# The second layer's output projection as seven block products, its weight blocks prepared during the first FFN

## The chip, the cores and the metric

The kernel runs on one core of one Trainium2 chip. The metric is the device time of one execution in microseconds (us), the median of several runs. The engines named below are PE (TensorE, the matrix multiplier), DVE (VectorE), ACT (ScalarE), POOL (GpSimd) and SP (SyncE); SP starts transfers on hardware queues, POOL starts them on a software queue, and only the latter are used here for transfers that add into their destination.

## The reference, cut to what matters

A decoder trunk of two layers on 1024 tokens with 1024 channels, all in float32. What matters here is the output projection `merged @ w_o[l]` and its surroundings:

```
for l in range(2):
    h = rmsnorm(x, norm1[l]);  proj = h @ w_in[l]          # q, k, v of two mixers, and two gates
    o_a, o_b = two attention mixers
    merged = g_a * (o_a @ w_br[l, :OUT_A]) + g_b * (o_b @ w_br[l, OUT_A:])
    x = x + merged @ w_o[l]                                 # 1024 x 1024 by 1024 x 1024
    h2 = rmsnorm(x, norm2[l]);  up = h2 @ w_up[l]           # 1024 x 5632
    x = x + (gelu(conv(a)) * v) @ w_down[l]                 # 2816 x 1024
return rmsnorm(x, norm_f)
```

## The kernel before, in words

**Arithmetic.** A float32 matrix product is made of three matmuls in PE's faster float32 format: each operand is split into a high part (a cast on ACT, `w_hi`, `hh`, `t_hi`) and a low part, the rest (a subtraction on DVE, `w_lo`, `hl`, `t_lo`; line 152 in `split`). Then hi·hi, hi·lo and lo·hi are added in one PSUM bank. One matmul has 128 weight columns against 512 tokens.

**Block products.** Most of the large products (the input projection, FFN up, FFN down) are already made in blocks of two by two, with seven block products and sums of blocks instead of eight block products. The output projection is not: `wo_chunk` makes one of 16 chunks, token half `n` by output block `e`, from 8 plain block pairs, thus 24 matmuls a chunk and 384 a layer. For each chunk, the weights of `w_o` are loaded (`w_raw`, two transfers of 256 KB), split on ACT and DVE, multiplied, and the result in PSUM is added to the residual `x` on DVE (line 1321). Then `norm_add` squares it on ACT and adds the square to `nrm` on DVE (line 491).

**The norm behind it.** When all eight chunks of a token half are done, four matmuls with `ones` (`nrm_t`) sum `nrm` over the channels, ACT and DVE make 1/sqrt of it (`ss`), and four matmuls (`nrm_b`) spread it over the partitions. DVE then scales `x` (`b_f`, line 563), ACT casts `hh` and DVE subtracts `hl`. In the second layer, `first_half()` does this for token half 0, and the sums of blocks for the FFN behind it (`s`, `t_hi`, `t_lo`), beside the chunks of half 1: `drive` mixes the two by a ratio. The norm of half 1 is left over as `pending` and is mixed into the first units of the FFN (`u_ps`).

**The branch stage ahead of it.** The two attention outputs go through `w_br` (`br_ps`), are multiplied by the gates (`gin`), added (`mrg`) and split: `hh` on ACT, `hl` on POOL (line 1419). Gates come from DRAM (`gs` to `gin`), as does the residual `x` (`xs`, 1 MB a transfer).

**The first FFN.** Units 2 to 21 of `up` make FFN up. Each unit has 84 matmuls in 14 steps of 6. In it, raw weights come by SP (`up_a<-in_w_up_dram`), are combined by DVE and by one adding transfer of POOL (line 1651, `up_a<-up_a`), are split on ACT and DVE, and ACT carries results out of PSUM (`u<-u_a`, `u<-u_c`) so that the bank can be used again.

**What sets the order.** Within these units PE, ACT, DVE and POOL run their instructions in the order of the program text (`IN_ORDER`); elsewhere a scheduler sets the order of ACT, DVE, POOL and SP, and SP's order throughout. Each engine runs its own list in order, and waits at the head of it.

Of the kernel before, what the change touches and what calls it, by code (L numbers as in the profile page):

```python
# [7 lines left out]
F32 = mybir.dt.float32  # L8
# [22 lines left out]
EPS = 1e-6  # L31
GRP = 2
NRAW = 2
PT = 6
WARM = 3
GROUPS = (2, 2, 3, 4)
# [23 lines left out]
def f32(ap):  # L60
    return ap.bitcast(F32)
# [3 lines left out]
def trunk_kernel(ctx, tc, x, xt, head0, norm1, vecs, w_in, w_br, w_o, w_up, w_down, norm_f, out, depth=None, probe=None):  # L65
# [57 lines left out]
    sq = [dr.tile([2, 2, 64, T], F32, name=f"sq{i}") for i in range(4)]  # L123
    sv = [dr.tile([P, n, KD, P], F32, name=f"sv{n}") for n in (4, 2, 2)]
    dn = [dr.tile([4, T], F32, name=f"dn{i}") for i in range(2)]
    fd = dr.tile([4, T], F32, name="fd")
# [62 lines left out]
    def drive(side, main, ratio, lead=0):  # L189

        due = 0.0
        for _ in range(lead):
            next(main, 0)
        for _ in side:
            due += ratio
            while due >= 1.0:
                due -= 1.0
                if next(main, 0) == 0:
                    due = -1e9
        for _ in main:  # L200
            pass
# [239 lines left out]
    def h_part(n, k):  # L441
        return H[n][0][:, k, :], H[n][1][:, k, :]
# [9 lines left out]
    def xc(n, e, sub=slice(0, HF)):  # L452
        return X[n][e // 4][:, e % 4, sub]
# [12 lines left out]
    def x_in(l, n, h):  # L466

        if h == 0:
            X[n] = [None, None]
        X[n][h] = quarter(f"x{n}")  # L470
        k = slice(4 * h, 4 * h + 4)
        if l:
            nc.sync.dma_start(X[n][h], xs[n][:, k, :])
        elif n:
            nc.sync.dma_start(X[n][h], x_first(1, HF, T)[:, k, :])
        else:
            for a in range(0, HF, 2 * P):
                nc.sync.dma_start(X[n][h][:, :, a : a + 2 * P], x_first(0, a, a + 2 * P)[:, k, :])
# [1 line left out]

    ACC = [None, None]

    def norm_add(n, e, first=False):

        if first:
            ACC[n] = sb.tile([P, HF], F32, tag="ql", bufs=2, name="nrm")
        acc = ACC[n]
        sq = acc if first else small("sq")
        act.activation(sq, xc(n, e), AF.Square)
        if not first:  # L490
            dve.tensor_tensor(acc, acc, sq, ALU.add)
# [824 lines left out]
    def wo_chunk(l, n, e):  # L1316
        w = weights(w_o[l][:, e * P : (e + 1) * P], P)
        yield
        o = bank("ps", "o_ps")
        yield from product(o, [(w[k], h_part(n, k)) for k in range(KD)])  # L1320
        dve.tensor_tensor(xc(n, e), xc(n, e), o, ALU.add)
        norm_add(n, e, e == 0)
        yield

    def mixer(l, pending):
        R.clear()
        dense = Dense()
# [79 lines left out]
        def branch_in(i):  # L1407
            if i < len(todo):
# [5 lines left out]
                    split(*parts_[q], raw[:, 2 * q : 2 * q + 2, :])  # L1414
                wbs.append(parts_)

        def merged(n, e, m):
            act.copy(H[n][0][:, e, :], m)
            pool.tensor_tensor(H[n][1][:, e, :], m, f32(H[n][0][:, e, :]), ALU.subtract)

        wo = [wo_chunk(l, n, e) for n in range(2) for e in range(KD)]

        for i in range(3):
            gate_load(i)
# [11 lines left out]
        for i, ab in order:  # L1436
            n, e = todo[i]
            sl = slice(n * HF, (n + 1) * HF)
            if i not in seen:
                if e == 0:  # L1440
                    new_h(n)
                if i % 4 == 0:
                    wb = wbs.pop(0)
                if i in X_AT:
                    late_x = X_AT.index(i)
                    x_in(l, late_x // 2, late_x % 2)
            gt = gts[i]
            ec = slice((e % 2) * P, (e % 2 + 1) * P)
            o = bank("s" if ab and i < 2 else (("ps", "s"), ("t", "o"))[ab][i // 2 % 2], "br_ps")
            (wh, wl), (xh, xl) = wb[ab], oh["ab"[ab]]  # L1450
            for _ in product(o, [((wh[:, c, ec], wl[:, c, ec]), (xh[:, c, sl], xl[:, c, sl])) for c in range(2)]):
                pass
            with tc.high_priority(offset=AHEAD):
                dve.tensor_tensor(gt[:, ab, :], gt[:, ab, :], o, ALU.mult)
            seen[i] = seen.get(i, 0) + 1
            if seen[i] == 1:
                continue
            m = small("mrg")
            dve.tensor_tensor(m, gt[:, 0, :], gt[:, 1, :], ALU.add)
            late.append((n, e, m))  # L1460
# [5 lines left out]
            if i == 12:  # L1466
                next(wo[0])
        merged(*late.pop(0))
        table(AF.Sqrt, gt[:, 1, 0:1])
# [2 lines left out]
        def first_half():  # L1472
            yield from norm(0, g2[:, 0, :], "t", keep=True)
            yield from first_sum()

        drive(first_half(), relay(*wo, primed=True), 2.5, 36)
        return norm(1, g2[:, 0, :], "t", AF.Gelu, True)

    def ffn(l, pending, final):
# [106 lines left out]
        def before(steps, n):  # L1586

            while now[1] < n and next(steps, 0) != 0:
                yield
# [12 lines left out]
        def up_weights(j, vv):  # L1602
            return weights(w_up[l][:, vv * DFF + j * P : vv * DFF + (j + 1) * P], P)

        def up_plain(j, order, turns, extra):

            yield
            yield
            w = [up_weights(j, 0), up_weights(j, 1)]
# [269 lines left out]
        for _ in steps:  # L1879
            pass  # L1880
        return box[0]

    heads = {}

    def enter(l):

# [457 lines left out]
```

## Time and profile before

| | before |
|---|---|
| median of 3 runs | 2594.13 us (2591.62 to 2595.03) |
| the profiled execution's own time | 2593.59 us |
| its span, first to last instruction | 2591.8 us |
| busy PE / DVE / ACT / POOL | 2577.4 / 2061.1 / 1334.1 / 130.0 us |
| granted TensorE clock | 1.0 |
| share of the DMA engines' time, hardware / software queue | 56.0% / 2.7% |

The profiled execution lies 0.54 us under the median, and 1.8 us of it lie outside the span. An engine's busy time is counted over the span, so PE was idle for 14.4 us in all. In the tables by stretch, each engine has its busy time and, in brackets, the number of its instructions; the last columns are the granted clock, the busy share of the 16 DMA engines, and GB/s. In a timeline a row has its start, its length and, in square brackets, the engine's idle time before it and what ended that.

### The profile page before, as it was taken

The page shows a single profiled execution, that of the slowest core. Times are in us where ns is not written, and L with a number is a line of the kernel's source. Part 1 is how long each engine was busy: PE and PEld are TensorE (multiplying, and loading weights), DVE is VectorE, ACT ScalarE, POOL GpSimd, SP SyncE. Part 2 cuts the span into 40 slices and gives each one's busy share as a digit, 9 for nine tenths or more (in the row PEclk, how much of TensorE's full clock was granted, in tenths as well). Part 3 has the DMA queues.
Part 4 walks back from the last instruction along what each step waited for, and adds up shares of the span by engine and source line. Part 5 has one row for each costly group of instructions (what it writes and reads, how often), then busy time and mean ns, then how long its engine had stood idle before and what let it go on. Part 6 is the DMA issues. An engine that isn't in the chain of part 4 may idle for free.

```text
span 2591.8 us, 35872 instructions
## 1 busy us (share of the span) xinstructions
PE 2577.4 (99%) x12536; PEld 2153.4 (83%) x12536; DVE 2061.1 (80%) x3410; ACT 1334.1 (51%) x2488; POOL 130.0 (5%) x175
## 2 busy tenths in 40 slices
PE   9999999999999999999999999999999999999999
PEld 8888888888888888888888888888888888888887
DVE  8878877796878878897677788778868888879966
ACT  6555566664554545432445555666645555544223
POOL 1000000030000000000000000000300000000000
PEclk9999999999999999999999999999999999999999
DMA  7434579863355455688344436798634455457963
GB/s 261 152 114 145 158 197 233 235 224 105 103 158 166 155 186 155 246 323 312 147 149 147 127 129 188 199 242 235 198 99 129 138 174 164 157 184 251 347 241 134
DMA packets 402579, 480.02 MB, mean 185 GB/s; under 512 B 25272, under 2 KB 311392, under 8 KB 400736
## 3 DMA queue, kind: packets, MB, share of 16 engines
q1 hardware_dynamic: 395776, 464.85, 56.0%
q0 software_dynamic: 6464, 12.62, 2.7%
q8 instruction: 99, 1.62, 0.3%
q14 instruction: 80, 0.66, 0.1%
q10 hardware_dynamic: 160, 0.27, 0.0%
HBM read 308.74 MB, written 158.43 MB: 180 GB/s over the span
## 4 chain that ended last, share of the span: by engine, by line
PE 92%; DVE 4%; ACT 2%; DMA 1%; issue 1%; POOL 0%; DVEq 0%; ACTq 0%; POOLq 0%
PE u_a L1053 5%; PE u_a L1052 5%; PE u_a L1054 5%; PE d_ps L1801 5%; PE d_ps L1802 5%; PE d_ps L1803 5%; PE i_a L1052 5%; PE i_a L1053 5%; PE i_a L1054 5%; PE u_c L1052 3%; PE u_c L1053 3%; PE u_c L1054 3%; PE i_c L1052 2%; PE i_c L1054 2%; PE i_c L1053 2%; PE o_ps L182 2%
## 5 line engine op out<-in xcount | busy, mean ns | idle before, releaser
L144 ACT CAST w_hi<-up_a 128x512 fp32r<-128x512 f32 x280 | 174.4, 624 | 265.1 <-DVE up_a L1658 133.4
L152 DVE TENSOR_TENSOR w_lo<-up_a,w_hi 128x512 fp32r<-128x512 f32 x280 | 189.4, 688 | 64.4 <-ACT w_hi L144 64.2
L144 ACT CAST w_hi<-in_a 128x512 fp32r<-128x512 f32 x252 | 156.2, 622 | 157.7 <-PE i_c L1053 33.6
L152 DVE TENSOR_TENSOR w_lo<-in_a,w_hi 128x512 fp32r<-128x512 f32 x252 | 173.1, 689 | 72.3 <-ACT w_hi L144 60.7
L1812 DVE TENSOR_TENSOR x<-x,d_ps 128x512 f32<-128x512 f32 x220 | 150.5, 685 | 59.5 <-PE d_ps L1803 56.3
L1052 PE MATMUL u_a<-hh,w_hi 128*128 128x512 f32 x320 | 124.5, 389 | 0.0
L1053 PE MATMUL u_a<-hl,w_hi 128*128 128x512 f32 x320 | 124.5, 389 | 0.0
L1054 PE MATMUL u_a<-hh,w_lo 128*128 128x512 f32 x320 | 124.5, 389 | 0.0
L1052 PE MATMUL u_a<-t_hi,w_hi 128*128 128x512 f32 x320 | 124.5, 389 | 0.0
L1053 PE MATMUL u_a<-t_lo,w_hi 128*128 128x512 f32 x320 | 124.5, 389 | 0.0
L1054 PE MATMUL u_a<-t_hi,w_lo 128*128 128x512 f32 x320 | 124.5, 389 | 0.0
L1801 PE MATMUL d_ps<-gd_in,w_hi 128*128 128x512 f32 x316 | 123.2, 390 | 0.0
L1802 PE MATMUL d_ps<-gd_in,w_hi 128*128 128x512 f32 x316 | 123.0, 389 | 0.0
L1803 PE MATMUL d_ps<-gd_in,w_lo 128*128 128x512 f32 x316 | 123.0, 389 | 0.0
L1052 PE MATMUL i_a<-hh,w_hi 128*128 128x512 f32 x288 | 117.8, 409 | 0.0
L1052 PE MATMUL i_a<-t_hi,w_hi 128*128 128x512 f32 x288 | 116.4, 404 | 0.0
L1054 PE MATMUL i_a<-t_hi,w_lo 128*128 128x512 f32 x288 | 113.0, 392 | 0.0
L1054 PE MATMUL i_a<-hh,w_lo 128*128 128x512 f32 x288 | 113.0, 392 | 0.0
L1053 PE MATMUL i_a<-hl,w_hi 128*128 128x512 f32 x288 | 112.9, 392 | 0.0
L1053 PE MATMUL i_a<-t_lo,w_hi 128*128 128x512 f32 x288 | 112.9, 392 | 0.0
L1801 PE MATMUL d_ps<-gd_in,wd 128*128 128x512 f32 x284 | 110.8, 390 | 0.0
L1803 PE MATMUL d_ps<-gd_in,wd 128*128 128x512 f32 x284 | 110.5, 389 | 0.0
(422 smaller groups left out, 7695.3 us busy)
## 6 DMA issues: line engine op xcount, KB each, us to landing
gd<-g SPq DMA_DIRECT2D x154, 512.0 KB, 3.4
gd_in<-gd SPq DMA_DIRECT2D x154, 512.0 KB, 6.2
up_a<-in_w_up_dram SPq DMA_DIRECT2D x80, 512.0 KB, 5.4
in_a<-in_w_in_dram SPq DMA_DIRECT2D x72, 512.0 KB, 5.4
wd_raw<-in_w_down_dram SPq DMA_DIRECT2D x22, 1024.0 KB, 9.5
gin<-gs SPq DMA_DIRECT2D x32, 512.0 KB, 4.5
w_raw<-in_w_o_dram SPq DMA_DIRECT2D x64, 256.0 KB, 2.9
gs<-u SPq DMA_DIRECT2D x48, 256.0 KB, 3.2
```

The lines of the kernel that those rows point to most:

```text
L144: one = act.copy(hi, src)
L152: two = dve.tensor_tensor(lo, src, f32(hi), ALU.subtract)
L182: pe.matmul(o, lh, rh, start=(first and i == 0), stop=False, skip_group_check=share)
L1052: pe.matmul(o, w[0][:, c], rh, start=(first and i == 0), stop=False, skip_group_check=True)
L1053: pe.matmul(o, w[0][:, c], rl, start=False, stop=False, skip_group_check=True)
L1054: pe.matmul(o, w[1][:, c], rh, start=False, stop=(last and i == 3), skip_group_check=True)
L1801: pe.matmul(o, wh[:, c], gh, start=(i == 0 and k in (0, 4, 5)), stop=False, skip_group_check=True)
L1802: pe.matmul(o, wh[:, c], gl, start=False, stop=False, skip_group_check=True)
L1803: pe.matmul(o, wl[:, c], gh, start=False, stop=(i == m - 1), skip_group_check=True)
L1812: dve.tensor_tensor(x, x, o, ALU.add)
```

## The change: what it does

The layers are numbered 0 and 1; `SEVEN = (1,)` names the second.

**In the first FFN**, `prepare(1)` makes the 28 weight blocks of the second layer's projection (7 products, 4 blocks of 128 x 512 each), one generator step after each step of `up` (276 steps beside the 280 of units 2 to 21, which it fills to the end). For a block it loads one tile by SP (`wo_n`, a single buffer), ACT multiplies it by a sign in place, which also makes it the high part, POOL writes it to DRAM (`wod[k, i][:, 0]`); three steps later ACT multiplies it by -1, POOL writes that, and POOL adds the float32 source onto it in DRAM, which leaves the low part. The sums of blocks (`wof`) are made by POOL's adding transfers alone. In all it adds 64 multiplications to ACT, 112 transfers to POOL's queue and 32 to SP's.

**In the second layer's branch stage**, sums of blocks of `merged` are made as it comes: 12 more DVE instructions (subtractions, low parts, sums), four fewer subtractions on POOL (12 instead of 16).

**The projection** (`out_proj`) is 7 products x 4 output blocks x 12 matmuls, 336 in all instead of 384, in the order 0, 4, 1, 2, 3, 5, 6. It loads the prepared parts (56 transfers of 256 KB, each product's when an earlier one has released its buffers), so that ACT's 32 casts and DVE's 32 subtractions of `w_o` go away; DVE makes 12 low parts `m_lo` and 8 sums `m_part`. Each product's four results are added to `x` (28 additions instead of 16). Three of the four 1 MB loads of `x` now stand between the weight loads. The norm of half 0 can begin only behind product 3, the fifth of seven: `nrm_t` stands 18 matmuls, and `nrm_b` 24 matmuls, into product 5. From that `nrm_t` to the one of half 1, PE has 84 matmuls, where it had 160.

```
@@ prepare(l)
+        def loaded(src):
+            t = sb.tile([P, HF], F32R, tag="bias", name="wo_n")
+            nc.sync.dma_start(f32(t), src)
+            return t
+        def halves(t, sign, k, i, src):
+            act.mul(t, f32(t), sign)
+            nc.gpsimd.dma_start(wod[k, i][:, 0, :], f32(t))
+            yield from (None,) * 3
+            act.mul(t, f32(t), -1.0)
+            nc.gpsimd.dma_start(wod[k, i][:, 1, :], f32(t))
+            nc.gpsimd.dma_start(wod[k, i][:, 1, :], src, accum_op=ALU.add)
+            yield from (None,) * 3
+        for i in range(4):
+            a11, a21, a12, a22 = (blocks_of(l, i)[x] for x in (0, 2, 1, 3))
+            nc.sync.dma_start(wof[sum_, i], a21)
+            nc.gpsimd.dma_start(wof[sum_, i], a22, accum_op=ALU.add)
+            for src, k, to in ((a11, 0, (turned, lift)), (a12, 4, (last,))):
+                t = loaded(src)
+                yield from (None,) * 3
+                act.mul(f32(t), f32(t), -1.0)
+                for s in to:
+                    nc.gpsimd.dma_start(wof[s, i], f32(t))
+                yield from (None,) * 3
+                yield from halves(t, -1.0, k, i, src)
+            nc.gpsimd.dma_start(wof[turned, i], a21, accum_op=ALU.add)
+            nc.gpsimd.dma_start(wof[lift, i], wof[sum_, i], accum_op=ALU.add, max_dma_last_dim=4 * HF)
+            nc.gpsimd.dma_start(wof[last, i], wof[lift, i], accum_op=ALU.add, max_dma_last_dim=4 * HF)
+            t = loaded(a22)
+            yield from (None,) * 3
+            yield from halves(t, 1.0, 3, i, a22)
+        for k, s in ((1, lift), (2, turned), (5, sum_), (6, last)):
+            for i in range(4):
+                t = loaded(wof[s, i])
+                yield from (None,) * 3
+                yield from halves(t, 1.0, k, i, wof[s, i])
...
@@ out_proj(l, keep)
+        order = (0, 4, 1, 2, 3, 5, 6)
+        into = ((0, 0), (1, 0), (1, 1), (0, 1), (0, 0), (1, 1), (1, 0))
...
+        def beside(k, e):
...
+            elif k == 4:
...
+                if e == 3:
+                    x_in(l, 1, 0)
+                    x_in(l, 1, 1)
+                    load(2)
...
+            elif k == 3:
+                square(0, 1, e, False)
...
+            for e in range(4):
+                o, c = banks[k][e], slice(e * P, (e + 1) * P)
+                for i in range(4):
+                    (wh, wl), (gh, gl) = ws[k][i], part(k, i)
+                    pe.matmul(o, wh[:, c], gh, start=(i == 0 and k in (0, 4, 5)), stop=False, skip_group_check=True)
+                    pe.matmul(o, wh[:, c], gl, start=False, stop=False, skip_group_check=True)
+                    pe.matmul(o, wl[:, c], gh, start=False, stop=(i == 3), skip_group_check=True)
...
+                    dve.tensor_tensor(x, x, o, ALU.add)
+                beside(k, e)
...
@@ mixer
-        drive(first_half(), relay(*wo, primed=True), 2.5, 36)
+        if seven_out:
+            side = first_half()
+            for n in (43, 0, 0, 1, 1):
+                for _ in range(n):
+                    next(wo)
+                next(side)
+            drive(side, wo, 1.0)
+        else:
+            drive(first_half(), relay(*wo, primed=True), 2.5, 36)
...
@@ ffn
+        ahead = prepare(l + 1) if l + 1 in SEVEN else iter(())
         with tc.manual_schedule(engines=IN_ORDER):
             for _ in before(steps, NF):
-                pass
+                next(ahead, None)
```

POOL, from the first layer's branch stage into the first FFN, before (`hl` is the low part in the branch stage, `up_a` the FFN's weights; `slots` and `beta` belong to the second layer's attention):

```order
L1419 TENSOR_TENSOR hl_5778<-mrg,hh_5777 128x512 x2
L1419 TENSOR_TENSOR hl_5796<-mrg,hh_5795 128x512 x2
L1651 DMA up_a<-up_a 128x512 x20
L677 MEMSET slots 64x4x256
L723 AFFINE_SELECT beta<-beta 128x128 x32
```

POOL in the first FFN after the change (the first two weight blocks; line 1843 is the old line 1651):

```order
L1843 DMA up_a<-up_a 128x512 x2
L1361 DMA wof<-wo_n 128x512 x2
L1345 DMA wod<-wo_n 128x512
L1348 DMA wod<-wo_n 128x512
L1349 DMA wod<-in_w_o_dram 128x512
L1843 DMA up_a<-up_a 128x512
L1361 DMA wof<-wo_n 128x512
L1345 DMA wod<-wo_n 128x512
L1348 DMA wod<-wo_n 128x512
L1349 DMA wod<-in_w_o_dram 128x512
L1364 DMA wof<-in_w_o_dram 128x512
L1365 DMA wof<-wof 128x512
```

Where POOL's list held nothing but the 20 adding transfers of the FFN's own weights, there now stand five or six transfers of the preparation to each of these on average, and some of them wait for the one ahead of them to land.

ACT in a unit of the first FFN, before (`u<-u_a` and `u<-u_c` empty a PSUM bank):

```order
L144 CAST w_hi<-up_a 128x512
L1674 COPY u_7464<-u_c 128x512
L144 CAST w_hi<-up_a 128x512
L1678 COPY u<-u_a 128x512
L144 CAST w_hi<-up_a 128x512
L144 CAST g<-cv 128x512
```

ACT there after the change:

```order
L1866 COPY u_7480<-u_c 128x512
L147 CAST w_hi<-up_a 128x512
L1870 COPY u<-u_a 128x512
L147 CAST w_hi<-up_a 128x512
L147 CAST g<-cv 128x512
L1344 ACTIVATE wo_n<-wo_n 128x512
L147 CAST w_hi<-up_a 128x512
L147 CAST g<-cv 128x512
L1347 ACTIVATE wo_n<-wo_n 128x512
```

The multiplications of `wo_n` stand between the casts and the copies that empty PSUM, and each waits at the head of ACT's list for its load (line 1344) or for the write of the high part (line 1347).

DVE at the end of the second layer's projection, before (`x` is the residual, `s` and `t_lo` are sums of blocks for the FFN and their low parts):

```order
L491 TENSOR_TENSOR nrm<-nrm,sq 128x512
L152 TENSOR_TENSOR w_lo<-w_raw,w_hi 128x512
L1321 TENSOR_TENSOR x_17919<-x_17919,o_ps 128x512
L152 TENSOR_TENSOR w_lo<-w_raw,w_hi 128x512
L536 TENSOR_TENSOR s_18622<-b_f_18546,b_f_18434 128x512
L491 TENSOR_TENSOR nrm<-nrm,sq 128x512
L152 TENSOR_TENSOR t_lo<-s_18622,t_hi 128x512
```

DVE there after the change, to the last addition to `nrm`, for which PE's `nrm_t` of half 1 waits:

```order
L1474 TENSOR_TENSOR x_18345<-x_18345,o_ps 128x512
L569 TENSOR_TENSOR hl_18663<-b_f_18727,hh_18662 128x512
L155 TENSOR_TENSOR t_lo<-s_18742,t_hi 128x512
L494 TENSOR_TENSOR nrm<-nrm,sq 128x512
L539 TENSOR_TENSOR s_18756<-b_f_18704,b_f_18664 128x512
L539 TENSOR_TENSOR s_18766<-b_f_18727,b_f_18681 128x512
L539 TENSOR_TENSOR s_18780<-b_f_18727,b_f_18681 128x512
L155 TENSOR_TENSOR t_lo<-s_18756,t_hi 128x512
L155 TENSOR_TENSOR t_lo<-s_18766,t_hi 128x512
L494 TENSOR_TENSOR nrm<-nrm,sq 128x512
L155 TENSOR_TENSOR t_lo<-s_18780,t_hi 128x512
L494 TENSOR_TENSOR nrm<-nrm,sq 128x512
```

The work on half 0 (`b_f`, `hl`, `s`, `t_lo`), which stood among the subtractions `w_lo` of the projection's weights, now stands as one block of 37 instructions from the first `b_f` to this last `nrm`: 8 scalings `b_f`, 8 `hl`, 4 `s`, 4 `t_lo`, 7 `nrm` and 6 additions to `x`.

More of the change, by code (lines that the diff above doesn't have):

```diff
@@ L33 @@
 NRAW = 2
+SEVEN = (1,)
 PT = 6
@@ L481, in trunk_kernel, with norm_add @@
     ACC = [None, None]
-    def norm_add(n, e, first=False):
+    def norm_add(n, e, first=False, room=None):
         if first:
-            ACC[n] = sb.tile([P, HF], F32, tag="ql", bufs=2, name="nrm")
+            ACC[n] = sb.tile([P, HF], F32, tag="ql", bufs=2, name="nrm") if room is None else room
         acc = ACC[n]
@@ L1323, in wo_chunk, with blocks_of, prepare @@
         yield
+    def blocks_of(l, i):
+        rows = [w_o[l][(2 * i + j) * P : (2 * i + j + 1) * P, :] for j in range(2)]
+        return [rows[j][:, f * HF : (f + 1) * HF] for f in range(2) for j in range(2)]
+    def prepare(l):
+        sum_, lift, turned, last = range(4)
+        def loaded(src):
[33 more added lines that the diff above has]
+                yield from halves(t, 1.0, k, i, wof[s, i])
@@ L1443, in mixer @@
                     wb = wbs.pop(0)
-                if i in X_AT:
+                if seven_out and i == 6:
+                    x_in(l, 0, 0)
+                elif not seven_out and i in X_AT:
                     late_x = X_AT.index(i)
@@ L1457, in mixer @@
                 continue
-            m = small("mrg")
-            dve.tensor_tensor(m, gt[:, 0, :], gt[:, 1, :], ALU.add)
-            late.append((n, e, m))
+            late.append(merge(i, gt))
             if len(late) > 1:
@@ L1465, in mixer @@
                 branch_in(i + 3)
-            if i == 12:
+            if seven_out and i == 9:
+                wo = out_proj(l, keep)
+                next(wo)
+            elif not seven_out and i == 12:
                 next(wo[0])
```

112 lines of the change are left out of this document (107 added, 5 removed).

## The prediction

> **What bounds the kernel now.** I read the page first, for the engine that is busy.
>
> ```profile
> span 2591.8 us, 35872 instructions
> PE 2577.4 (99%) x12536; PEld 2153.4 (83%) x12536; DVE 2061.1 (80%) x3410; ACT 1334.1 (51%) x2488; POOL 130.0 (5%) x175
> ```
>
> PE is busy in all but 14.4 us. A matmul less is time less, as long as nobody makes PE wait instead; the change can lose more than it gains only by new waits of PE. So I next read PE's waits around the projection, and then the stretches: the branch stage (to 1855), the projection (1855 to 1944), the norm and first FFN units behind it, and two stretches of the first FFN, where the preparation goes.
>
> ```profile
> PE u_c L1052 <- ACT u L1674: 1.0, 1, 1.0
> PE o L658 <- DVE p1l L152: 0.3, 1, 0.3
> ```
>
> ```profile
> core 0: us, PE busy (x) PEld busy (x) DVE busy (x) ACT busy (x) POOL busy (x), PEclk, DMA share, GB/s
> 1811.00:1855.00 44.00, 44.00 (x196) 36.44 (x195) 42.29 (x57) 29.95 (x50) 17.28 (x12) 1.00 0.82 277
> 1855.00:1900.00 45.00, 44.93 (x199) 36.89 (x198) 27.54 (x39) 18.92 (x32) 5.18 (x4) 1.00 0.31 90
> 1900.00:1946.00 46.00, 46.00 (x210) 38.20 (x209) 32.70 (x53) 20.55 (x36) 0.00 (x0) 1.00 0.32 92
> 1946.00:1960.00 14.00, 14.00 (x68) 11.51 (x67) 12.68 (x23) 7.83 (x13) 0.91 (x1) 1.00 0.44 112
> 900.00:950.00 50.00, 50.00 (x222) 41.43 (x221) 41.03 (x62) 26.11 (x42) 1.77 (x2) 1.00 0.52 162
> 1050.00:1090.00 40.00, 40.00 (x178) 33.11 (x177) 34.62 (x51) 20.28 (x32) 0.87 (x1) 1.00 0.64 225
> ```
>
> The clock is 1.00 in each. In the projection everything but PE has room: DVE 27.54 of 45 us, DMA 0.31. At its edges it has not: ahead of it DVE works 42.29 of 44 us and the DMA engines 0.82; behind it DVE 12.68 of 14. In the first FFN the DMA share is 0.52 to 0.64, and ACT about half busy.
>
> **The change part by part.** The sum is made against the profiled execution, 2593.59 us (0.54 under the median).
>
> **Matmuls.** 384 become 336. From 1855 to 1900, 199 matmuls filled 45.00 us, 0.226 us each: 48 x 0.226 = 10.85 us less. That is the whole gain; ACT's 32 casts and DVE's 32 subtractions of `w_o` were not waited for.
>
> **Start of the projection.** DVE gets 12 instructions more in the branch stage, about 6 of them ahead of the merge (`mrg`) that feeds the last `hl` of product 0.
>
> ```profile
> 1853.18 1.29 DVE L1459 TENSOR_TENSOR mrg<-gin 128x512 f32<-128x512 f32 x1
> 1854.94 0.39 PE L182 MATMUL o_ps<-hh,w_hi 128*128 128x512 f32 x1
> 1855.20 1.29 POOL L1419 TENSOR_TENSOR hl<-mrg,hh 128x512 fp32r<-128x512 f32 x1 [1.28 <-ACT hh L1418]
> ```
>
> Product 0 wants this `hl` with its ninth matmul, 2.0 us after its start (1856.97), and it is ready at 1856.49: 0.5 us to spare. The 5 subtractions `w_lo` that stood there go, so the net delay is one or two instructions of 0.6 to 1.3 us. I take 0.8 us; from 0 up to 4 (six instructions at 0.7, nothing saved). Below nothing is excluded, since PE has no wait there to lose.
>
> **Loads during the projection.** Transfers issued from 1811 to 1946, with KB each and the median us from issue to landing:
>
> ```profile
> w_raw<-in_w_o_dram SPq DMA_DIRECT2D x32, 256.0 KB, 2.9
> ...
> gs<-u SPq DMA_DIRECT2D x1, 256.0 KB, 5.8
> gs<-last SPq DMA_DIRECT2D x1, 256.0 KB, 4.2
> ```
>
> 56 parts of 256 KB are 14.7 MB instead of 8.4, plus 3.1 MB of `x`, in 78 us: 230 GB/s on the mean, and about 300 in products 4 and 1, where two `x` loads stand in SP's list ahead of load(2). In the branch stage the engines carried 277 GB/s at a share of 0.82, and a `w_raw` came in 2.9 us on the median. A product's loads have one product, 10.85 us, to land: 2.1 MB at 277 GB/s is 7.6 us. I take 0.2 us, between 0 and 4 (one late x and one late set).
>
> **Norm of half 1.** This is the largest new wait. The rows of today:
>
> ```profile
> 1939.12 0.69 DVE L152 TENSOR_TENSOR w_lo<-w_raw,w_hi 128x512 fp32r<-128x512 f32 x1
> 1939.72 0.69 DVE L536 TENSOR_TENSOR s<-b_f,b_f 128x512 f32<-128x512 f32 x1
> 1940.32 0.68 DVE L491 TENSOR_TENSOR nrm<-nrm,sq 128x512 f32<-128x512 f32 x1
> 1945.76 0.69 DVE L491 TENSOR_TENSOR nrm<-nrm,sq 128x512 f32<-128x512 f32 x1
> 1946.60 1.02 PE L546 MATMUL nrm_t<-ones,nrm 128*128 128x1 f32 x8
> 1950.30 0.60 PE L555 MATMUL nrm_b<-ident,ss 128*128 128x128 f32 x4
> 1950.93 1.41 DVE L563 SCALAR_TENSOR_TENSOR b_f<-x,vec,nrm_b 128x512 f32<-128x512 f32 x2 [1.11 <-PE nrm_b L555]
> ```
>
> `nrm_t` starts 0.15 us after the last `nrm` has ended; DVE's instructions follow each other every 0.60 us, `b_f` every 0.70. After the change, DVE must get through the block of 37 from the first `b_f` of half 0 to the last `nrm` of half 1: 8 x 0.70 + 29 x 0.60 = 23.0 us. Count from the end of product 3. PE: 18 matmuls 4.07, `nrm_t` 1.02, 6 matmuls 1.36, `nrm_b` 0.60, then 78 matmuls 17.63: it stands at `nrm_t` of half 1 after 24.7 us. DVE: `nrm_b` starts at 6.45, the first `b_f` 0.63 later at 7.08, the block ends at 30.1, and 0.35 later because its last addition to `x` needs the last matmul of product 6 (23.35) where DVE alone would be there at 23.0. PE waits 30.5 - 24.7 = 5.8 us. Against that, five instructions (`s`, `t_lo`) that today stand behind the last `nrm` are then done, so DVE is 3 us further ahead, and the 1.0 us wait at `u_c` should go; 0.15 us of wait is there today. Net 5.8 - 1.0 - 0.15 = 4.65 us, from 0 (rival 1) to 8 (if the block also waits for ACT's casts and squares, some five times 0.7). `nrm_t` of half 0 has its `nrm` 2.3 us after product 3, ahead of 4.07, and costs nothing.
>
> **Preparation in the first FFN.** A simple block takes 9 steps of 6 matmuls, 9 x 6 x 0.226 = 12.2 us. Within it stands a chain: multiply, write of the high part lands, multiply, write of the low part lands, next load lands. The durations:
>
> ```profile
> L144 ACT CAST w_hi<-up_a 128x512 fp32r<-128x512 f32 x280 | 174.4, 624 | 265.1 <-DVE up_a L1658 133.4
> up_a<-up_a POOLq DMA_DIRECT2D x18, 256.0 KB, 3.3
> w_raw<-in_w_in_dram SPq DMA_DIRECT2D x1, 256.0 KB, 3.1
> up_a<-in_w_up_dram SPq DMA_DIRECT2D x36, 512.0 KB, 5.5
> L1651 POOL DMA_DIRECT2D up_a<-up_a x40: 861/874/924, 670.4 to 2333.9; - x40
> ```
>
> An ACT multiplication is like the cast, 0.62; POOL's nearest transfer of that size lands 3.3 us after issue; the load takes 3.1 alone, 5.5 if it shares with the 512 KB loads in front of it in SP's queue. So 0.62 + 3.3 + 0.62 + 3.3 + 3.1 = 10.9 us, 1.3 under the period. The second multiplication waits for the first write: 3.3 + 0.62 = 3.9 us against 3 steps, 4.07. Close, but in time. What queues behind it: ACT's copies out of PSUM and casts, DVE's subtractions behind those casts, then PE.
>
> ```profile
> 904.28 0.39 PE L1054 MATMUL u_a<-t_hi,w_lo 128*128 128x512 f32 x1
> 904.70 0.59 ACT L1678 COPY u<-u_a 128x512 f32<-128x512 f32 x1 [1.09 <-PE u_a L1054]
> 907.22 0.39 PE L1052 MATMUL u_a<-t_hi,w_hi 128*128 128x512 f32 x1
> 914.89 0.87 POOL L1651 DMA_DIRECT2D up_a<-up_a  x1 [16.39 <-DMA up_a<-in_w_up_dram]
> 926.24 0.62 ACT L144 CAST w_hi<-up_a 128x512 fp32r<-128x512 f32 x1 [0.87 <-PE u_c L1053]
> ```
>
> The bank is free at 905.29 and wanted at 907.22, so ACT may be 1.9 us late at no cost. POOL's wait for a write delays `up_a<-up_a` by up to 3.3 us; issued at 914.89 it has landed at 918.2, and the earliest cast that may read it is at 926.24, 8 us of room. ACT's 64 x 0.62 = 40 us lie in its free half. The added traffic, about 1.1 MB per 12.2 us, is 90 GB/s on top of 162: the share goes from 0.52 to about 0.8. The four blocks that read `a22` stand behind three adding transfers in a row, where ACT may wait 2 us each. I take 0.6 us for all; below nothing is excluded, PE having no idle time there. Above: with the 5.5 us load and both writes at the 4.2 us of `gs<-last` (with `gs<-u` the only writes from SBUF to DRAM of this size there, both in the crowded branch stage), the chain is 15.1 us, 2.9 too long, 28 times: 82 us. I stay near the low end because `up_a<-up_a` is a transfer of POOL's own queue in this same stage, and the two writes are of another queue at a share of 0.82.
>
> The Trainium skill, "DMA: Bandwidth & Descriptors", section "Anatomy of one DMA", gives a transfer of the software queue as 2.0 us plus bytes over 436 GB/s. For 256 KB that would be 2.6 us, where the row has 3.3; by it the chain would be 9.5 us and the term 0. I go by the row.
>
> Sum: -10.85 + 0.8 + 0.2 + 4.65 + 0.6 = -4.6 us: 2593.59 - 4.6 = 2589.0 us.
>
> **The rivals.**
> 1. The norm's wait is given back: DVE, relieved of the `w_lo` of `w_o`, comes out of it with its FFN work ahead, and PE meets no wait where it would have. For it: DVE is 80% busy over the span, yet PE's only wait behind the projection is 1.0 us. Against: the block of 37 is counted, and no part of it can be left out before `nrm_t`. Time: 2593.59 - 10.85 + 1 = 2583.7.
> 2. The other side: the chain of the preparation is longer than its period and paces PE. It decides at 12.2 us a block, 1.3 us over my sum; that is reached if the load takes 4.4 instead of 3.1, or the two writes 3.95. For it: the DMA share there is already 0.52 to 0.64 and grows to 0.8, and at 0.82 the two writes of 256 KB took 4.2 and 5.8 us; the load shares SP's queue with 512 KB loads. Against: `up_a<-up_a` landed in 3.3 on the median in this very stage. At 13.0 us a block, 0.8 x 28 = 22 us: 2611.
> 3. The transfers of the projection come late, products 2 and 1 wait 2 to 6 us: 2593. For: 300 GB/s is wanted there, more than the 277 of the branch stage. Against: 2.9 us for `w_raw` at that load.
> 4. POOL's issues are held up by DVE, which is 82% busy in this stage (41.03 of 50 us): one DVE instruction, 0.69 us, on each of the two writes makes the chain 10.9 + 1.4 = 12.3, 0.1 x 28 = 3 us: 2592. Against: 861 to 924 ns over 40 issues beside that same DVE load. This is what the Trainium skill, "SBUF — State Buffer", warns of in its box on the software queue: GpSimd can't write descriptors while a DVE instruction in a two-port mode holds the shared port. By these 40 rows it doesn't happen with this DVE work.
>
> **How the numbers follow.** A change of 0.2%, 5.2 us (2588.9 and 2599.3 about the median), is about what the measurement can tell from none. My forecast, 2589.0, has 0.40; its own range is 2585 to 2594, by the bounds of its terms, and it lies on the border: 0.22 faster, 0.18 same. Rival 1 has 0.19, all faster. Rival 2 has 0.25: 0.21 slower, 0.04 same. Rival 3 has 0.11: 0.07 same, 0.04 slower (with more than one late set). Rival 4 has 0.05: same 0.03, faster 0.02. Faster 0.43, same 0.32, slower 0.25. The range reaches from rival 1's 2582 (under which some 0.05 lie) to 2613, which takes in rival 2 up to 13 us a block and leaves about 0.13 above.
>
> **What would show it.** PE's matmuls of the projection from first to last about 78 us, waits apart. In PE's waits: `nrm_t` of half 1 for DVE `nrm`, 4 to 7 us, and no `u_c` wait behind it. A wait of `o_ps` for `hl` at product 0 of about 1 us; `o_ps` for `wo_in` none. In the first FFN: ACT idle ahead of the `wo_n` multiplications, ended by transfers, each under 2 us, the landings of `wod<-wo_n` about 3.3 us, and PE without a wait on `u_a` or `u_c`. I am wrong if the first FFN grows: units of more than 84 x 0.226 = 19.0 us mean rival 2. If the `nrm_t` wait is under 1 us it is rival 1, and if PE waits for `wo_in` rival 3.

## The result, and the profile after

The changed kernel takes 2684.01 us in the median of 4 runs (2680.98 to 2689.68), the kernel before 2593.85 beside it: a ratio of 1.0351, 95% interval 1.033 to 1.0373, 90 us slower. The forecast was 2589.0, with a range from 2582 to 2613. The profiled execution has a span of 2679.2 us, 87.4 more than before. From the page of the changed kernel, and from the stretches of both kernels between the same landmarks (first FFN up in two parts, FFN down, all up to the projection, the projection, the first two FFN units behind it):

```profile
span 2679.2 us, 36097 instructions
PE 2595.9 (97%) x12488; PEld 2155.5 (80%) x12488; DVE 2062.2 (77%) x3422; ACT 1350.3 (50%) x2532; POOL 204.4 (8%) x283
```

Changed kernel:

```profile
702.60:930.00 227.40, 193.88 (x786) 153.70 (x785) 141.53 (x209) 104.42 (x175) 47.15 (x67) 0.92 0.71 200
930.00:1170.80 240.80, 212.36 (x896) 169.56 (x895) 165.17 (x244) 119.83 (x200) 43.94 (x63) 0.96 0.77 222
1170.80:1383.70 212.90, 211.51 (x934) 174.10 (x935) 173.65 (x278) 69.82 (x115) 0.88 (x1) 1.00 0.73 271
1383.70:1945.70 562.00, 557.67 (x3022) 471.93 (x3022) 447.49 (x814) 331.15 (x697) 36.06 (x50) 1.00 0.63 183
1945.70:2023.20 77.50, 77.50 (x349) 64.34 (x348) 55.30 (x87) 25.39 (x42) 4.26 (x3) 1.00 0.62 207
2023.20:2076.00 52.80, 48.02 (x202) 39.52 (x201) 44.23 (x78) 25.37 (x44) 0.86 (x1) 0.90 0.19 55
```

Before:

```profile
705.10:892.00 186.90, 186.33 (x822) 153.99 (x821) 150.65 (x224) 97.00 (x155) 7.86 (x9) 1.00 0.51 161
892.00:1086.70 194.70, 194.70 (x860) 161.22 (x859) 157.85 (x232) 99.92 (x157) 7.90 (x9) 1.00 0.55 175
1086.70:1297.80 211.10, 210.92 (x936) 174.19 (x936) 171.59 (x274) 69.23 (x115) 0.00 (x0) 1.00 0.72 267
1297.80:1854.90 557.10, 556.22 (x3022) 471.96 (x3021) 443.86 (x804) 330.80 (x697) 37.67 (x52) 1.00 0.64 185
1854.90:1943.80 88.90, 88.83 (x398) 73.32 (x398) 58.30 (x87) 38.23 (x65) 5.18 (x4) 1.00 0.31 91
1943.80:1988.20 44.40, 44.40 (x203) 36.67 (x202) 41.74 (x73) 24.67 (x41) 1.78 (x2) 1.00 0.38 106
```

FFN up, which has the preparation beside it, went from 381.6 to 468.2 us: +86.6. FFN down +1.8, the way to the projection +4.9, the projection -11.4 (77.5 for 88.9), the first units behind it +8.4; the rest, and an earlier start of FFN up, is -2.9. The same 1682 matmuls lie in both FFN-up stretches. PE stood still there for 62 us, and it was busy for 406.2 us instead of 381.0. Of these 25 us about 16 are the granted clock, 0.92 and 0.96 in the two parts: behind some of the pauses 76 matmuls follow each other every 0.43 us instead of every 0.227. The other 8 to 9 us, an estimate from the same spacings, go with starting again after 27 pauses.

What PE waited for in FFN up, and what ACT and SP waited for (us in total, times, longest):

```profile
PE u_a L1055 <- ACT u L1862: 25.7, 15, 7.9
PE u_a L1055 <- ACT u L1870: 21.5, 4, 10.4
PE u_c L1055 <- ACT w_hi L147: 7.2, 1, 7.2
PE u_c L1055 <- ACT u L1866: 6.2, 7, 2.3
```

```profile
ACT wo_n L1347 <- DMA wod<-wo_n: 118.7, 26, 16.3
ACT wo_n L1344 <- DMA wof<-wo_n: 29.0, 7, 8.4
```

```profile
SPq L1340 <- DMA wod<-wo_n: 156.1, 24, 18.2
```

PE waits for ACT to empty PSUM banks; ACT stands at the second multiplication of a block until the first write has landed; SP stands at the next block's load until the second write has landed. (The line of L1344 is the same wait in the first blocks, whose high parts also go to the sums `wof` out of the one tile.) One block, in the timelines of ACT, POOL and SP (the two multiplications and the next block's first, the writes and the adding transfer ahead of them, the next load):

```profile
1075.50 0.63 ACT L1344 ACTIVATE wo_n<-wo_n 128x512 fp32r<-128x512 f32 x1 [1.26 <-DMA wo_n<-wof]
1083.47 0.63 ACT L1347 ACTIVATE wo_n<-wo_n 128x512 fp32r<-128x512 f32 x1 [6.31 <-DMA wod<-wo_n]
1090.24 0.62 ACT L1344 ACTIVATE wo_n<-wo_n 128x512 fp32r<-128x512 f32 x1
...
1073.36 0.85 POOL L1349 DMA_DIRECT2D wod<-wof  x1 [2.68 <-DMA wod<-wo_n]
1076.49 0.56 POOL L1345 DMA_DIRECT2D wod<-wo_n  x1 [2.27 <-ACT wo_n L1344]
1084.51 0.54 POOL L1348 DMA_DIRECT2D wod<-wo_n  x1 [7.46 <-ACT wo_n L1347]
...
1087.05 0.32 SPq L1340 DMA_DIRECT2D wo_n<-wof  x1
```

From the first multiplication to the second 7.97 us, to the next load 3.58, to the next block 3.19: 14.7 us, where PE at full clock gives the block 12.2. Over the 15 plain blocks from 953 us on, the median from one block's first multiplication to the next one's is 14.6. The first write is the long link. All first and all second writes of the second half of FFN up (930 to 1200), with their time from issue to landing (min/median/max):

```profile
L1345 POOL DMA_DIRECT2D wod<-wo_n x17: 559/568/1107, 939.9 to 1162.3; - x17
...
DMA to landing us min/median/max: 2.3/5.4/7.8
```

```profile
L1348 POOL DMA_DIRECT2D wod<-wo_n x17: 539/555/567, 946.1 to 1170.2; - x17
...
DMA to landing us min/median/max: 2.3/2.3/6.9
```

The same transfer lands in 2.3 us or in 5.4: the first is issued 3.1 us after an adding transfer from DRAM to DRAM, which takes 6.8 us on the median, and lands behind it. All of FFN up says the same: 24 of its 56 writes `wod<-wo_n` were issued while another transfer of POOL's queue was under way, and each of these landed after that transfer, 4.7 us from its issue on the median; for the other 32 the median is 2.4. The Trainium skill, "DMA: Bandwidth & Descriptors", section "SWDGE vs HWDGE vs iDMA", says that the software path has only one queue; these figures agree with transfers that stand in line there.

### The profile page after: what moved, and what is told of

Same layout as the page of the kernel before. It is cut to its first block, busy times and chain, and to the rows that moved or that the text cites. A ratio compares the mean times of both kernels' runs of the same rounds, so it can differ in the third digit from the quotient of the medians.

```text
span 2679.2 us, 36097 instructions
## 1 busy us (share of the span) xinstructions
PE 2595.9 (97%) x12488; PEld 2155.5 (80%) x12488; DVE 2062.2 (77%) x3422; ACT 1350.3 (50%) x2532; POOL 204.4 (8%) x283
## 5 line engine op out<-in xcount | busy, mean ns | idle before, releaser
L147 ACT CAST w_hi<-in_a 128x512 fp32r<-128x512 f32 x252 | 156.2, 622 | 157.8 <-PE i_c L1056 33.5
L1055 PE MATMUL u_a<-t_hi,w_hi 128*128 128x512 f32 x320 | 131.9, 412 | 47.3 <-ACT u L1862 25.7
L1055 PEld LDWEIGHTS u_a<-t_hi,w_hi 128*128 128x128 f32 x320 | 62.7, 196 | 69.2 <-ACT u L1862 32.7
L155 DVE TENSOR_TENSOR g<-cv,g 128x512 fp32r<-128x512 f32 x154 | 105.5, 685 | 14.4 <-ACT g L147 14.4
```

The source lines that it names most:

```text
L147: one = act.copy(hi, src)
L155: two = dve.tensor_tensor(lo, src, f32(hi), ALU.subtract)
L1055: pe.matmul(o, w[0][:, c], rh, start=(first and i == 0), stop=False, skip_group_check=True)
```

## The experiments

FFN up is measured from the first `u_a` matmul to the first `d_ps` matmul in the profiled execution, 381.6 us before and 468.2 after. Each ratio is against the kernel before, run on the same chip in between.

**a1_no_prep: the projection without the preparation.** The edit leaves one block in `prepare` and lets every load read it:

```
-                    nc.sync.dma_start(f32(ws[k][i][h]), wod[k, i][:, h, :])
+                    nc.sync.dma_start(f32(ws[k][i][h]), wod[3, 0][:, h, :])
```

> Leaves out the preparation of 27 of the 28 weight blocks: all 56 loads of the projection read one prepared block, so the second layer's values are not the reference's; the instructions of the projection and its traffic stay. If the whole loss is made in the first FFN (the theory), that FFN is back at 382 us and only the second layer's differences remain: branch stage and what lies ahead of it +4.9, projection -11.4, norm and first units +8.4, together 2593.85 + 2 = about 2596, within 2592 to 2599. If part of the 90 us came from the projection itself, it stays above 2610.

Measured: 2594.28 us, ratio 1.0004 (0.9995 to 1.0013); FFN up 382.9 us. So the loss is the preparation's, and the seven products alone gain nothing that can be measured: what the matmuls save is spent around them (b1 and b6 below win it back).

**a2_prep_only: the preparation without the projection** (`seven_out = False`).

> The preparation as in the change, but the second layer's projection plain, as before. If the loss lies in the preparation alone: the first FFN takes about 468 us instead of 382, total 2593.85 + 86 to 88 = 2680 to 2682. If the preparation costs only because the rest of the change is there (other order of the loads), under 2640.

Measured: 2683.39 us, ratio 1.0347 (1.0331 to 1.0363); FFN up 469.8 us. The two parts add up.

**a3_no_mul: all transfers, no multiplications** (the three `act.mul` lines removed).

> The change without its 64 multiplications on ACT: all loads, writes and adding transfers stay, so that ACT waits for none of them (the prepared weights are then wrong). Theory, ACT's list held by waits for transfers: the first FFN is back at 382 to 390 us, total 2595 to 2604. Rival, the traffic itself (0.77 of the transfer engines' time) or POOL's list holding back the FFN's own adding transfer: the first FFN stays over 420 us, total over 2635.

Measured: 2681.53 us, ratio 1.0340 (1.0326 to 1.0354); FFN up 466.6 us. The theory as I had put it fell: with ACT waiting for none of the preparation's transfers, nothing is won. The waits of SP and of ACT in this kernel show where the chain went:

```profile
SPq L1340 <- DMA wod<-wo_n: 308.1, 30, 24.0
```

```profile
ACT g L147 <- DMA gd<-g: 86.8, 29, 9.6
ACT w_hi L147 <- DMA up_a<-up_a: 50.5, 10, 6.6
```

SP's list is run in order too. Its wait at the next load, 156 us in the changed kernel, is now 308 us, and behind that load stand the FFN's own stores `gd<-g`, whose buffers ACT needs, and the loads of its weights. POOL's list waits as well here, and in a4 below it does so too, where most of the loss is gone; so SP's list is the likelier carrier in this kernel, which no run shows apart from POOL's.

**a4_own_tiles: the whole computation, high and low part in tiles of their own** from the pool of six, so that no load and no multiplication waits for a write of its block. (The high part stays in the tile of the load, except in the first eight blocks, which write it to the sums `wof` as well.)

```
-            t = sb.tile([P, HF], F32R, tag="bias", name="wo_n")
+            t = small("wo_n", F32R)
...
+            hi, lo = t if fresh else small("wo_h", F32R), small("wo_l", F32R)
+            act.mul(hi, f32(t), sign)
...
+            act.mul(lo, f32(hi), -1.0)
```

> The whole computation; the preparation writes the high part and the low part from tiles of their own (the pool of six 128 x 512 tiles that the FFN leaves idle) instead of one tile in place, so that no multiplication waits for a write to land. ACT keeps its 64 multiplications, which wait only for loads. Theory: ACT's 118.7 + 29 us of waits for writes go, the waits for loads (26 us, mostly under the 1.9 us of slack) go too since the next load no longer waits for a write: first FFN 382 to 395 us, total 2595 to 2610. Rival (traffic, or POOL's list): as a3, over 2635.

Measured: 2614.02 us, ratio 1.0080 (1.0067 to 1.0094); FFN up 395.9 us. Both numbers lie just above what was expected. Of 86.6 us, 72 are gone with the same transfers and the same multiplications. So it was the reuse of the one tile at this pace, felt by two lists. The 14 us that stay are no waits of ACT or SP for a write: POOL's list still waits for the writes in front of its adding transfers, 138 us in all, and a5 below, which moves these, takes the rest.

**b4_act_waits: a tile per block, still worked on in place** (only the first of the lines above): SP is free, ACT still waits.

> The change with one word altered: each block is loaded into a tile of the rotating pool of six instead of the one tile, and is still worked on in place. So SP's load no longer waits for the write of the block before (156 us of SP's waits in the changed kernel), but ACT's second multiplication still waits for the first write to land (119 us). It is the counterpart of a3_no_mul, in which ACT waits for nothing, SP still does, and the first FFN stayed at 467 us. If each of the two lists holds PE by itself: the first write lands 5.4 us after its issue and 7 us after the first multiplication, 2.9 beyond the three steps, 1 us beyond ACT's slack, 28 to 36 times: first FFN 410 to 450 us, total 2620 to 2665. If SP's list alone holds PE: as a4_own_tiles, first FFN about 396 us, total 2608 to 2616.

Measured: 2673.22 us, ratio 1.0304 (1.0287 to 1.0322); FFN up 457.1 us, 7 above the expected span. ACT's waits for `wod<-wo_n` were 119.3 us, as in the changed kernel; SP's wait at `wo_n` was down from 156 to 3.1 us. With a3 this shows, POOL's waits left aside, that each of the two lists alone holds PE nearly as long as both.

**b3_adds_last: the one tile, the 28 adding transfers of the low parts at the end.**

```
-            nc.gpsimd.dma_start(wod[k, i][:, 1, :], src, accum_op=ALU.add)
+            owed.append((wod[k, i][:, 1, :], src))
```

> The change with its one tile, in place, three steps a stage; only the 28 adding transfers that make the low parts are issued after all blocks, beside the start of FFN down. In the changed kernel the first write of a block, issued while the adding transfer of the block before is under way (6.8 us on the median), lands after 5.4 us, the second after 2.3. Theory: without an adding transfer ahead of it the first write lands in 2.3 to 3 us too, the chain is 14.8 - 3 = 11.8 us, under the period of 12.2: first FFN 382 to 405 us, total 2598 to 2625 (with something lost in FFN down to the 28 transfers). Rival, the one tile and its waits are enough to lose the time whatever the writes take: first FFN over 440 us.

Measured: 2666.95 us, ratio 1.0293 (1.0278 to 1.0309); FFN up 425.2 us, between the two expectations, and FFN down 241 us instead of 211 beside the 28 transfers. From 930 on the first writes landed in 3.2 us on the median instead of 5.4, and PE was busy for 229 of 235 us:

```profile
704.00:930.00 226.00, 200.08 (x823) 159.99 (x822) 151.19 (x223) 111.88 (x187) 41.18 (x60) 0.95 0.69 205
930.00:1165.00 235.00, 229.45 (x996) 187.04 (x996) 186.01 (x275) 123.56 (x203) 35.48 (x53) 0.99 0.76 244
```

So the adding transfer in front of the write is what makes the chain too long in the second half (which here reaches into FFN down). In the first half, where the sums `wof` are made by adding transfers as well, most of the loss stays, 26 us of idle PE where the changed kernel has 33.5.

**a8_steps5: five steps a stage instead of three**, 20.3 us a block, the rest beside FFN down.

> The change with one number altered: five steps instead of three between the stages of a block, in the one tile, so that a block has 20.3 us instead of 12.2; what does not fit beside FFN up goes on beside FFN down. The chain measured in the changed kernel is 8.0 us from the first multiplication to the second (its write lands behind the adding transfer of the block before), 3.6 to the next load and 3.2 to the next block: 14.8 us. If the chain against its period is what costs: each stage then has 6.8 us, the first is late by 1.2, under ACT's slack of 1.9: first FFN 382 to 400 us, total 2595 to 2625. If any waiting instruction in ACT's and SP's lists costs whatever its spacing: first FFN over 430 us.

Measured: 2638.07 us, ratio 1.0178 (1.0164 to 1.0192); FFN up 400.0 us, at the edge of what was expected. The total is above it, because FFN down took 235.4 us instead of 211: ACT's 13 waits for `wod<-wo_n` there last 47.0 us, and PE stands 11.7 us at one `nrm_t`. That these waits are what makes it longer is a reading; no run separates them. In FFN up the same reused tile costs 18 us at 20.3 us a block, where it costs 87 at 12.2.

**a5_late_adds: a4_own_tiles with the adding transfers later in POOL's list.**

```
-            nc.gpsimd.dma_start(wod[k, i][:, 1, :], src, accum_op=ALU.add)
             yield from (None,) * 3
+            nc.gpsimd.dma_start(wod[k, i][:, 1, :], src, accum_op=ALU.add)
```

The adding transfer that makes the sum `last` also moves, behind the block read from `a22`.

> As a4_own_tiles, and POOL issues each adding transfer three steps later, so that POOL does not stand waiting for the write to land while the FFN's own adding transfer (up_a) is behind it in POOL's list; the sum `last` is added after the block of a22. If what a4 still lost in the first FFN (396 us instead of 382) is POOL's list holding up_a back: first FFN 382 to 388 us, total 2598 to 2604. If it is the traffic (0.94 of the transfer engines' time from 800 to 900): no change, 2610 to 2618.

Measured: 2594.46 us, ratio 1.0005 (0.9995 to 1.0014); FFN up 382.5 us. FFN up came as expected; the total lies under what was expected, and equals that of a1_no_prep. The preparation is free now. It runs at a higher load than in the changed kernel:

```profile
703.90:930.00 226.10, 225.53 (x993) 185.86 (x992) 181.90 (x269) 136.43 (x225) 59.01 (x83) 1.00 0.92 261
930.00:1086.40 156.40, 156.25 (x691) 129.08 (x689) 127.24 (x187) 93.15 (x151) 31.86 (x46) 1.00 0.87 257
```

With 0.92 of the transfer engines' time taken, 261 GB/s, PE loses 0.6 us in 226. Traffic, the other explanation, was not it: the changed kernel had 0.71 in that half and lost 33.5 us to idle alone.

**a6_norm_later and a7_no_prep_norm_later: the second norm later** (`drive(pending, before(steps, 2), 0.7, 5)` in the second layer). In a6, some sums of half 1 are then taken ahead of the scaling that makes their blocks, so it is not the reference's computation.

> As a5_late_adds, and the second layer's norm of half 1 is started 30 matmuls into the first FFN unit instead of 12 (5 steps ahead instead of 2), 4.1 us later, when DVE's last addition to nrm is nearly done. Theory: PE's 4.8 us wait at nrm_t falls under 1.5 us and the lower clock behind it (0.90 over 53 us) goes: 6 to 8 us less than a5_late_adds. Rival, the wait only moves to the first matmuls on half 1: the same as a5_late_adds.

> As a1_no_prep (one prepared block read for all, second layer's values not the reference's), with the later norm of a6_norm_later. Theory: 6 to 8 us under a1_no_prep, 2586 to 2589, so that the seven products gain what is left of 10.85 us once PE does not wait behind them. Rival: 2594 as a1_no_prep.

Measured: 2596.55 us, 1.0010 (1.0002 to 1.0019), and 2595.60 us, 1.0009 (1.0000 to 1.0018). The totals are as in a5 (2594.46), so neither kernel shows the gain that was expected. Nothing follows on the norm itself: the wait at `nrm_t` fell from 4.8 to 0.7 us and the first units from 51.8 to 47.5, but the scheduler also ordered ACT's and DVE's work in the attention stage anew, and the way from FFN down to the projection took 567.8 instead of 560.9.

**b1_norm_30: the same with the attention stage untouched** (ratio 0.45, 5 steps).

> As a5_late_adds, with the norm of half 1 started 30 matmuls into the first FFN unit instead of 12, and the scaling of half 1 mixed in faster (ratio 0.45 instead of 0.7) so that it ends at the same step; the lists of the attention stage, which a6_norm_later had changed as well, stay as in a5_late_adds. In a5 PE waits 4.8 us there and then runs at a granted clock of 0.54 to 0.60 for about 7 us. Theory: the wait falls to about 0.7 us, no lower clock: 4.1 us of waiting and some 3 us of slow matmuls less, 2587 to 2590. Rival: the wait moves to nrm_b or to the first matmuls on half 1: 2593 to 2595.

Measured: 2588.63 us, ratio 0.9984 (0.9976 to 0.9993), the first version faster than the kernel before. The first units took 46.6 us instead of a5's 51.8: 5.2 us less for a wait that is 4.1 us shorter (4.8 to 0.7). Most of the rest is the clock, see below: the slow matmuls behind the wait cost 1.9 us in a5 and 0.6 here, an estimate from their spacing.

**b2_pool_lows and b5_branch_early: DVE's load in the branch stage.** b2 gives four low parts back to POOL, b5 starts the branch weights one item earlier (`i % 4 == 0`, `branch_in(i + 4)`).

> As b1_norm_30, and four low parts of the branch stage are made by POOL, as before the change, instead of DVE. PE waits 2.8 us there for DVE (br_w), and the stage ahead of the projection takes 560.9 us in a5_late_adds where it took 557.1. Theory, DVE's list is the bound of that stage: 2 to 3 us less than b1_norm_30. Rival, POOL's instructions (1.3 us each) stretch DVE's beside them, or product 0 waits for them: same or up to 3 us more.

> As b1_norm_30, and the second layer's branch weights (br_w) are loaded and split one item earlier. In b1 PE waits 3.1 us for DVE's br_w in the branch stage and then runs about 5 us at a granted clock of 0.54 to 0.78; the stage ahead of the projection takes 564.3 us where it took 557.1. Theory: the subtraction of br_w stands behind DVE's new instructions in its list, one item (2.7 us of PE) earlier is nearly enough: wait under 1 us, no lower clock, 2582 to 2585. Rival, DVE is the bound there and the wait comes at the next operand: 2587 to 2590.

Measured: 2588.96 us, 0.9986 (0.9977 to 0.9995), and 2589.02 us, 0.9987 (0.9978 to 0.9996): no change against b1. In b2 PE waited 4.0 us for `br_w` instead of 3.1, in b5 2.3 us. Both theories fell: less work for DVE and earlier weights each win nothing.

**b6_branch_first: the splits of the branch weights ahead in the scheduler's order** (`tc.high_priority` around them).

> As b1_norm_30, with the splits of br_w put ahead in the scheduler's order instead of loaded earlier. Theory as for b5_branch_early: 2582 to 2586. Rival: what is put behind (the products with the gates, which free PSUM) makes PE wait instead: 2587 to 2595.

Measured: 2585.40 us (2583.92 to 2587.78), ratio 0.9975 (0.9965 to 0.9985). That is within what was expected. It beats both kernels: 7 us under the one before, 99 under the changed one. The stretch in question, in b5 and in b6:

```profile
1830.00:1845.00 15.00, 12.65 (x49) 9.76 (x48) 14.26 (x21) 10.95 (x19) 4.71 (x4) 0.89 0.81 274
```

```profile
1830.00:1845.00 15.00, 15.00 (x68) 12.43 (x67) 14.07 (x22) 11.55 (x19) 4.34 (x4) 1.00 0.76 252
```

49 matmuls against 68 in the same 15 us, with DVE equally busy: it was the order in DVE's list, not its load. PE waits no more for `br_w`. It now waits for POOL's `hl` of product 0, at the place and with the size that the prediction gave for the changed kernel:

```profile
PE o_ps L1468 <- POOL hl L1597: 0.8, 1, 0.8
```

## Why the prediction was wrong, point by point

**The preparation in the first FFN** is the step that failed: +0.6 us forecast, +86.6 measured. Rival 2 named the mechanism, the place and the point from which it decides (12.2 us a block, or writes of 3.95 us), with a chance of 0.25. Three things in the working were off.
- The first write was priced at 3.3 us by the nearest transfer of the same queue. It lands in 5.4, because the adding transfer of the block before is ahead of it. Each part had a row; that they stand in one line was not asked. The second write takes 2.3. From a multiplication to the issue of its write it is 1.0 us, not 0.62. So a block took 14.6 us on the median, not 10.9.
- A chain was compared with its period. But PE is the bound, and a list run in order gives nothing back: a stage that comes 3 us late holds ACT and, beyond 1.9 us, PE; a stage that comes early earns nothing. Each stage had to fit its own 4.07 us. (This is read from the waits; a8 goes with it, whose stages have 6.8 us each and which lost 18 us in FFN up instead of 87.) I had set the second multiplication against that (3.9 against 4.07) and called it close but in time.
- The upper end worked out there, 82 us, was close to what came, but by luck: it counts 5.5 us for a load and 4.2 for each write, which took 2.8, 5.4 and 2.3, and no clock, and PE's pauses alone came to 62. I left it out of the range by giving more than 13 us a block hardly any chance.

**The clock** was not in the sum at all. The longer pauses of PE are followed by slow matmuls: in FFN up all five pauses of 3.1 us or more (to 10.4), and two of the 22 shorter ones (1.9 and 2.6 us). PE's timeline around its wait at `nrm_t` in the changed kernel:

```profile
2025.72 0.39 PE L187 MATMUL u_ps<-hh,w_lo 128*128 128x512 f32 x1
2030.89 1.84 PE L549 MATMUL nrm_t<-ones,nrm 128*128 128x1 f32 x8 [4.78 <-DVE nrm L494]
2032.59 0.77 PE L185 MATMUL u_ps<-hh,w_hi 128*128 128x512 f32 x1
2033.16 0.63 PE L186 MATMUL u_ps<-hl,w_hi 128*128 128x512 f32 x1
2033.59 0.63 PE L187 MATMUL u_ps<-hh,w_lo 128*128 128x512 f32 x1
...
2038.84 0.39 PE L186 MATMUL u_ps<-hl,w_hi 128*128 128x512 f32 x1
2039.07 0.40 PE L187 MATMUL u_ps<-hh,w_lo 128*128 128x512 f32 x1
```

```profile
2031.00:2034.00 3.00, 3.00 (x11) 2.72 (x12) 0.18 (x1) 1.22 (x2) 0.00 (x0) 0.50 0.00 0
2034.00:2038.00 4.00, 4.00 (x11) 3.01 (x10) 0.00 (x0) 0.62 (x2) 0.00 (x0) 0.50 0.01 4
```

After 4.8 us of standing still, matmuls follow each other every 0.43 us instead of 0.226, at a granted clock of 0.50, for 7 us, which costs some 3 us more. In FFN up, beside 62 us of pauses, this cost about 16. The Trainium skill, "TensorE: Matmul & The Clock Gate", "Part 1: The HAM clock gate", says that the clock is halved after an idle window of about 3.4 us and comes back after a busy window of about 3.4 us; the halving agrees, but pauses of 3.1, 2.6 and 1.9 us brought it too, and the way back took about twice that here.

**The matmuls**: -10.85 forecast, -11.4 in the stretch. Right.

**The norm of half 1**: a wait of 5.8 us forecast, 4.8 measured, at the place named, behind DVE's last `nrm`. Part of the missing 1.0 us is a count: PE has 90 matmuls between the two `nrm_t` in this trace, not 84, and with 90 the same sum gives 4.4. The wait at `u_c` fell from 1.0 to 0.5 us. The mechanism was right, and the term (4.65 net) too small: the first units take 8.4 us more, some 3 of them by the clock. b1 won 5.2 us of it back.

**The start of the projection**: 0.8 us forecast at product 0's `hl`, none there (b6 has it); instead PE waited 3.3 us for `br_w`, earlier in the same stage, where DVE's new instructions stand ahead of its subtraction. With it the way to the projection is 4.9 us longer. b6 shows that the order carries it: there the way takes 558.4 us, where it took 557.1 before and 562.0 in the changed kernel.

**The loads of the projection**: no wait of PE for `wo_in`, as forecast. **POOL's issues** (rival 4): 539 to 567 ns for the second writes beside a busy DVE (the highest in all of FFN up is 579); no sign of it, as the row had said. The issues of `up_a<-up_a` on the same list did grow, from about 870 to 1094 ns on the median, and were 896 in a5; what lengthens them no run shows.

The sum without the preparation was -5.2 us. a1_no_prep has it at +1 (2594.28), b6_branch_first, with the preparation free, the wait for `br_w` gone and that at `nrm_t` down to 0.7 us, at -7.0. That it comes near -5.2 is in part luck, since b6 has the later norm, which the predicted kernel has not.

## What to carry to other kernels

Where work is hidden beside a bound engine, price it by lists, not by averages: each in-order list that an added instruction enters (here ACT's, SP's and POOL's) must meet every one of its waits within that list's slack, and one tile reused in place ties all of them to the landing of each transfer. Taking one waiting list out of the chain may change nothing, since the next list in line carries the same wait; what has to go is the reuse at that pace: tiles of their own (a4) did it, and a longer period (a8) did most of it in FFN up. And before a transfer is priced by the nearest row, look at what was issued just ahead of it on its queue.

## What the runs showed of the hardware that I had not expected

- A write of 256 KB from SBUF to DRAM on POOL's queue lands in 2.4 us on the median of 32 that were issued with nothing else of that queue under way, and in 4.7 on the median of 24 issued behind another transfer; all 24 landed after it. An adding transfer between two places in DRAM takes 6.8 us on the median.
- In the changed kernel a pause of PE of 4.8 us is followed by some 7 us at half the clock; behind a pause of 3.1 us in b1_norm_30 the granted clock was 0.54 and 0.78 in the next two stretches of 5 us.
- In a5_late_adds the transfer engines were busy for 0.92 of the time over 226 us beside a PE that stayed busy for 225.5 of them.
